# Chaining the token-stationary products of an encoder block on TensorE in program order

## The chip, the cores and the metric

The kernel runs on one core of a Trainium2 chip. The metric is the device time of one execution in microseconds (us), the median of several runs.

## The reference

One layer of a streaming encoder with 256 tokens of width 2048, in float32. What matters here is the sequence of large matrix products:

```python
x = x + 0.5 * swiglu(rms_norm(x), ffn1_w_gate, ffn1_w_up, ffn1_w_down)   # 2048 -> 5632 -> 2048
proj = rms_norm(x) @ w_in                                                # 2048 -> 4112
x = x + concat([pool_mixer(...), gla_mixer(...)]) @ w_out                # 2048 -> 2048
x = x + mem_cross_attention(rms_norm(x), rms_norm(mem), w_q, w_kv, w_o)  # 256 memory tokens
x = x + 0.5 * swiglu(rms_norm(x), ffn2_w_gate, ffn2_w_up, ffn2_w_down)
return rms_norm(x)
```

`swiglu(h, g, u, d)` is `(silu(h @ g) * (h @ u)) @ d`.

## The kernel before

**Precision.** Each float32 operand is split into a high and a low part in the type that TensorE takes at full rate: ScalarE casts the high part (`wh`, L247), VectorE subtracts it from the operand for the low part (`wl`, L248). One float32 product then is three TensorE products: low times high, high times low and high times high. In `products` (L330) the stationary side is 128 tokens of an activation (`act`) and the moving side 512 columns of a weight, so these blocks are called token-stationary.

**Units.** The weights stream through SBUF in units of 1 MB. `Stream` keeps a list of units and of small operations to be put between them (`op(f, after=n)` puts f behind n more units). `emit` walks the list: it splits the weights of the unit that lies two ahead, then traces the products of the present one. There are three buffers each for the raw weights, `wh` and `wl`.

**Two kinds of units in a block.** `block_t` and `block_b` use plain units of 24 products. `block_s`, which makes two column blocks of 512 for all 256 tokens, mixes plain units (`unit_p`, 24 products at L330) with Strassen units (`unit_s`, seven block products P1 to P7 of three TensorE products each, 21 products at L454 in `seven`). For the Strassen units VectorE forms sums of weights (`T`, L431) and of activations (`Sums`). P2, P3 and P4 go straight into the result's sums; P1, P5, P6 and P7 go into two more PSUM tiles that `combine` adds up (L516 to L519) after the last Strassen unit of the block. The first Strassen unit of a block has the order P1, P7, P5, P6, P2, P3, P4.

**PSUM.** All of it is one pool of four tiles of two banks (`ptile`, tag `ps`). A `block_s` takes two for the result (`open_whole`) and two for the parts (`open_parts`, with the first Strassen unit).

**Blocks that add into x.** `into_x` runs two such blocks, b = 0 and 1, for the two halves of the 2048 columns. When the half's sums are complete, `residual` (L699) adds them to x; if a norm follows (`gain` is given), two calls of `fold` per half transpose the new x on TensorE (L722, eight transposes each, into a PSUM tile `px`), and ScalarE (L216) and VectorE (L217) copy that tile out into `xs`, by turns for each quarter of it. For the first half these copies are not tied to the order of the weights' splits. The folds of the first half are put one unit behind the half:

```python
for j in range(2):
    st.op(lambda c=2 * b + j: fold(c, gain), 1)
```

so they stand behind the first unit of the second half. Three calls of `into_x` have folds: the last part of the first layer's down projection (`REST`), `w_out` and `w_o` (both `OUTPUT`). In the second half `OUTPUT` has the units in the order 1, 0, 2, 3, 4, 5, 6, 7, with 0 and 4 Strassen units, and `REST` has 1, 2, 0, 3, 4, 5 with 0 a Strassen unit.

**Who orders the instructions.** The program is traced in the order above, and the framework's scheduler then orders each engine's queue: it plays the program through with its own estimate of durations and gives each engine, whenever it is free, the first instruction in traced order whose inputs are ready by that estimate. An order can be forced: `in_turn(engine, f)` puts an instruction behind the one that it last recorded for this engine (`latest`), without a wait for its end. The splits of the weights are forced so on ScalarE and VectorE, and `among_weights` and `behind_weights` put other operations behind those. TensorE's queue is free: in the kernel before, the scheduler takes a product of a later unit ahead when it finds the next one not ready.

Of the kernel before, what the change touches and what calls it, by code (L numbers as in the profile page):

```python
# [90 lines left out]
def build(ctx, tc, I, out):  # L91
    nc = tc.nc
# [132 lines left out]
    def in_turn(engine, f):  # L225

        if engine in latest:
            with tc.issue_after(latest[engine].ins):
                latest[engine] = f()
        else:  # L230
            latest[engine] = f()
# [93 lines left out]
    def products(ps, act, k, h, wh, wl, first, last):  # L325

        tok = slice(h * P, (h + 1) * P)
        parts = [(act[:, k, 0, tok], wh), (act[:, k, 0, tok], wl), (act[:, k, 1, tok], wh)]
        for i, (a, w) in enumerate(parts):
            nc.tensor.matmul(ps, a, w, start=first and i == 0, stop=last and i == 2)  # L330

    def block_t(srcs, act, evict, delays=(0, 0), amid=None):

        n_k = 2 * len(srcs)
        held = {}

        def unit(gi):
            def fn(wh, wl):  # L340
                if gi == 0:
                    held["ps"] = [ptile(uid("pt")) for _ in range(2)]
                wh, wl = (w.rearrange("p (k j n) -> p k j n", j=2, n=NB) for w in (wh, wl))
                quarters = [(j, kk) for j in range(2) for kk in range(2)]
                if amid is not None and gi == 0:
                    quarters.sort(key=lambda q: q[1])
                for n, (j, kk) in enumerate(quarters):
                    if amid is not None and n == (1 if gi else 3):
                        amid(gi)
                    k = 2 * gi + kk  # L350
                    for h in range(2):
                        products(held["ps"][j][:, h, :], act, k, h, wh[:, kk, j], wl[:, kk, j],
                                 k == 0, k == n_k - 1)
            return fn

        for gi, src in enumerate(srcs):
            st.unit(src, unit(gi))
        for j in range(2):
            st.op(lambda j=j: evict(j, held["ps"][j]), delays[j])
# [80 lines left out]
    def seven(banks, act, sums, g, fresh, ends, weights, order):  # L440
        th, tl, rh, rl = weights
        k0, k1, lo, hi = 2 * g, 2 * g + 1, slice(0, P), slice(P, S)
        a11, a12, a22 = ([act[:, k, p, t] for p in range(2)] for k, t in ((k0, lo), (k1, lo), (k1, hi)))
        s3, n1, n4, s2 = sums.parts(g)
        table = {
            "P1": (a11, rh[:, 0], rl[:, 0]), "P3": (n4, rh[:, 1], rl[:, 1]),
            "P2": (a12, rh[:, 2], rl[:, 2]), "P5": (n1, th[:, 0], tl[:, 0]),
            "P7": (s3, th[:, 1], tl[:, 1]), "P6": (s2, th[:, 2], tl[:, 2]),
            "P4": (a22, th[:, 3], tl[:, 3]),
        }  # L450
        for n in order:
            (a, b), wh, wl = table[n]
            for j, (x, w) in enumerate(((a, wh), (a, wl), (b, wh))):
                nc.tensor.matmul(  # L454
                    banks[n], x, w, start=n in fresh and j == 0, stop=n in ends and j == 2
                )

    def block_s(srcs, act, sums, order, evict, merge=None, sevens=None, late=0):

# [21 lines left out]
        def unit_s(g):  # L481
            def fn(weights):
                if g == sevens[0]:
                    open_parts()
                open_whole()
                fresh = {f"P{i}" for i in range(1, 8)} - seen
                seen.update(fresh)
                ends = ("P1", "P5", "P6", "P7") if g == sevens[-1] else ()
                if "P1" in fresh:
                    order = ("P1", "P7", "P5", "P6", "P2", "P3", "P4")  # L490
                elif merge:
                    order = ("P1", "P2", "P4", "P3", "P5", "P6", "P7")
                else:
                    order = ("P1", "P2", "P3", "P7", "P5", "P6", "P4")
                seven(held["banks"], act, sums, g, fresh, ends, weights, order)
            return fn

        def unit_p(g):
            def fn(wh, wl):
                open_whole()  # L500
                wh, wl = (w.rearrange("p (k j n) -> p k j n", j=2, n=NB) for w in (wh, wl))
                for j in (1, 0):
                    for h in range(2):
                        n = names[j, h]
                        for kk in range(2):
                            products(held["banks"][n], act, 2 * g + kk, h, wh[:, kk, j],
                                     wl[:, kk, j], n not in seen and kk == 0,
                                     g == order[-1] and kk == 1)
                        seen.add(n)
            return fn  # L510
# [35 lines left out]
    def block_b(srcs, act, evict, delay=0):  # L546

        n_k = 4 * len(srcs)
        held = {}

        def unit(gi):
            def fn(wh, wl):
                if gi == 0:
                    held["ps"] = ptile(uid("pb"))
                wh, wl = (w.rearrange("p (k n) -> p k n", n=NB) for w in (wh, wl))
                for kk in range(4):
                    k = 4 * gi + kk
                    for h in range(2):
                        products(held["ps"][:, h, :], act, k, h, wh[:, kk], wl[:, kk],
                                 k == 0, k == n_k - 1)  # L560
            return fn

        for gi, src in enumerate(srcs):
            st.unit(src, unit(gi))
        st.op(lambda: evict(held["ps"]), delay)
# [926 lines left out]
```

## Time and profile before

| | |
|---|---|
| median of 3 runs | 2102.96 us (2101.17 to 2103.69) |
| the profiled execution | 2102.94 us |
| its span, first to last instruction | 2101.2 us |
| mean granted TensorE clock | 0.998 |
| busy: TensorE, VectorE, ScalarE | 99%, 83%, 53% |
| moved from HBM | 417.58 MB, 207 GB/s over the span |

In the lines of a page PE is TensorE, PEld its weight loads, DVE VectorE, ACT ScalarE, SP the queue that issues the weight DMAs. A row of a timeline has the start from the span's beginning, the duration of the row, engine, source line, operation, output and inputs by tile name, how many instructions the row merges, and in brackets the idle time before it with what ended it. A row of the waits has the waiting group, what it waited for, the sum in us, how often, and the longest. A row of a table by windows has the stretch, its length, the busy time and count of PE, PEld, DVE, ACT and POOL, the granted TensorE clock, the busy share of the DMA engines and GB/s.

### The profile page before, as it was taken

The page shows a single profiled execution, that of the slowest core. Times are in us where ns is not written, and L with a number is a line of the kernel's source. Part 1 is how long each engine was busy: PE and PEld are TensorE (multiplying, and loading weights), DVE is VectorE, ACT ScalarE, POOL GpSimd, SP SyncE. Part 2 cuts the span into 40 slices and gives each one's busy share as a digit, 9 for nine tenths or more (in the row PEclk, how much of TensorE's full clock was granted, in tenths as well). Part 3 has the DMA queues.
Part 4 walks back from the last instruction along what each step waited for, and adds up shares of the span by engine and source line. Part 5 has one row for each costly group of instructions (what it writes and reads, how often), then busy time and mean ns, then how long its engine had stood idle before and what let it go on. Part 6 is the DMA issues. An engine that isn't in the chain of part 4 may idle for free.

```text
span 2101.2 us, 24556 instructions
## 1 busy us (share of the span) xinstructions
PE 2084.1 (99%) x9898; PEld 1741.7 (83%) x9898; DVE 1737.5 (83%) x1578; ACT 1118.8 (53%) x1100; POOL 13.1 (1%) x41
## 2 busy tenths in 40 slices
PE   9999999999999999999999999999999999999998
PEld 7878888888888788888888888888888888888886
DVE  7999899989998777678766455779998999989974
ACT  7655455645554545455645444456554556545544
POOL 0000000000000000000000000000000000000001
PEclk9999999999999999999999999999999999999999
DMA  7556666566656565467754555656566755676673
GB/s 261 202 199 224 237 220 216 185 223 249 213 197 236 191 198 183 158 192 242 262 185 161 163 174 165 219 184 227 190 227 211 245 202 191 225 240 220 206 257 118
DMA packets 143608, 435.94 MB, mean 207 GB/s; under 512 B 9860, under 2 KB 13544, under 8 KB 143112
## 3 DMA queue, kind: packets, MB, share of 16 engines
q1 hardware_dynamic: 143464, 434.38, 61.5%
q8 instruction: 77, 1.26, 0.2%
q14 instruction: 35, 0.29, 0.0%
q10 hardware_dynamic: 32, 0.01, 0.0%
HBM read 417.58 MB, written 16.78 MB: 207 GB/s over the span
## 4 chain that ended last, share of the span: by engine, by line
PE 92%; DVE 5%; issue 2%; ACT 1%; DMA 0%; SPq 0%; DVEq 0%; ACTq 0%
PE pt L330 43%; PE pt L454 21%; PE pa L315 14%; PE pb L330 6%; PE pe L330 3%; DVE wl L248 1%; DVE T L431 1%; PE ph L807 1%; DVE wl L435 1%; DVE xl L248 1%; PE pl L1226 1%; PE pv L1261 1%; ACT wh L247 1%; PE px L722 0%; DVE sg L531 0%
## 5 line engine op out<-in xcount | busy, mean ns | idle before, releaser
L248 DVE TENSOR_TENSOR wl<-raw,wh 128x2048 fp32r<-128x2048 f32 (+2 forms) x278 | 624.0, 2250 | 215.8 <-ACT wh L247 215.1
L247 ACT CAST wh<-raw 128x2048 fp32r<-128x2048 f32 (+2 forms) x278 | 521.2, 1880 | 318.5 <-PE pt L330 83.1
L330 PE MATMUL pt<-wh,xs 128*128 128x512 f32 x1536 | 494.9, 390 | 0.1
L330 PE MATMUL pt<-wh,ys 128*128 128x512 f32 x1344 | 423.4, 390 | 0.0
L434 ACT CAST wh<-T 128x1024 fp32r<-128x1024 f32 x208 | 218.8, 1053 | 347.4 <-DVE T L431 340.8
L330 PEld LDWEIGHTS pt<-wh,xs 128*128 128x128 f32 x1536 | 287.5, 188 | 59.4 <-ACT xs L216 0.4
L315 PE MATMUL pa<-xs,wh 128*128 128x512 f32 x896 | 317.4, 399 | 2.7 <-ACT wh L247 2.5
L330 PE MATMUL pt<-wl,xs 128*128 128x512 f32 x768 | 299.7, 390 | 0.0
L330 PEld LDWEIGHTS pt<-wh,ys 128*128 128x128 f32 x1344 | 251.9, 188 | 52.3 <-ACT wh L247 0.4
L330 PE MATMUL pt<-wl,ys 128*128 128x512 f32 x672 | 261.6, 389 | 0.0
L315 PE MATMUL pa<-xs,wl 128*128 128x256 f32 x896 | 248.4, 281 | 0.0
L435 DVE TENSOR_TENSOR wl<-T,wh 128x2048 fp32r<-128x2048 f32 x104 | 237.6, 2285 | 1.0 <-ACT wh L434 0.8
L315 PEld LDWEIGHTS pa<-xs,wh 128*128 128x128 f32 x896 | 168.1, 189 | 41.8 <-ACT wh L247 3.2
L248 DVE TENSOR_TENSOR xl<-raw,xh 128x1536 fp32r<-128x1536 f32 x104 | 182.2, 1752 | 13.6 <-ACT xh L247 13.6
L315 PEld LDWEIGHTS pa<-xs,wl 128*128 128x128 f32 x896 | 169.8, 190 | 2.1 <-issue 0.2
L330 PEld LDWEIGHTS pt<-wl,xs 128*128 128x128 f32 x768 | 144.2, 188 | 29.9
L247 ACT CAST xh<-raw 128x1536 fp32r<-128x1536 f32 x104 | 153.9, 1480 | 24.2 <-PE pt L454 13.4
L431 DVE TENSOR_TENSOR T<-T,raw 128x512 f32<-128x512 f32 x208 | 143.7, 691 | 5.8
L330 PEld LDWEIGHTS pt<-wl,ys 128*128 128x128 f32 x672 | 126.2, 188 | 26.2
L431 DVE TENSOR_TENSOR T<-raw 128x1024 f32<-128x1024 f32 x104 | 126.9, 1220 | 0.5
L454 PE MATMUL pt<-wh,xs 128*128 128x512 f32 x320 | 124.6, 389 | 0.0
L454 PE MATMUL pt<-wh,xe 128*128 128x512 f32 x320 | 124.5, 389 | 0.0
(236 smaller groups left out, 2430.6 us busy)
## 6 DMA issues: line engine op xcount, KB each, us to landing
raw<-in_ffn_w_down SPq DMA_DIRECT2D x88, 1024.0 KB, 5.6
raw<-in_ffn_w_up SPq DMA_DIRECT2D x80, 1024.0 KB, 5.0
raw<-in_ffn_w_gate SPq DMA_DIRECT2D x77, 1024.0 KB, 5.1
raw<-in_w_in SPq DMA_DIRECT2D x32, 1024.0 KB, 5.3
raw<-in_xattn_w_kv SPq DMA_DIRECT2D x32, 1024.0 KB, 5.2
raw<-in_w_out SPq DMA_DIRECT2D x16, 1024.0 KB, 5.7
raw<-in_xattn_w_q SPq DMA_DIRECT2D x16, 1024.0 KB, 5.7
raw<-in_xattn_w_o SPq DMA_DIRECT2D x16, 1024.0 KB, 5.6
```

What stands on the lines that cost most here:

```text
L247: in_turn("scalar", lambda: nc.scalar.copy(hi, src))
L248: in_turn("vector", lambda: nc.vector.tensor_tensor(out=lo, in0=src, in1=f32(hi), op=ALU.subtract))
L315: nc.tensor.matmul(o, w, x, start=k == 0 and i == 0, stop=last and i == 1)
L330: nc.tensor.matmul(ps, a, w, start=first and i == 0, stop=last and i == 2)
L431: in_turn("vector", lambda: nc.vector.tensor_tensor(out=o, in0=a, in1=b, op=ALU.add))
L434: in_turn("scalar", lambda: nc.scalar.copy(th[:, c], t[:, c]))
L435: in_turn("vector", lambda: nc.vector.tensor_tensor(out=tl, in0=t, in1=f32(th), op=ALU.subtract))
L454: nc.tensor.matmul(banks[n], x, w, start=n in fresh and j == 0, stop=n in ends and j == 2)
L807: nc.tensor.transpose(v[:, i, h * P : (h + 1) * P], g[:, h, i * P : (i + 1) * P], ident)
L1226: nc.tensor.matmul(ps[:, t, :M], ys[:, 4 * h + d, a, tok], xa["K"][:, d, b, :], start=i == 0, stop=i == 11,)
L1261: nc.tensor.matmul(ps[:, d, :S], xa["V"][:, m, a, col], xa["PT"][:, m, b, :], start=i == 0, stop=i == 5,)
```

## The change

The products of `products` (called by `block_t`, `block_s`, `block_b` and the last down projection) and of `seven` are queued on TensorE with `in_turn`, each behind the one traced before it. `block_a`, whose stationary side is the weight, the transposes and the attention's products are not touched.

```diff
@@ -327,7 +327,9 @@
         tok = slice(h * P, (h + 1) * P)
         parts = [(act[:, k, 0, tok], wh), (act[:, k, 0, tok], wl), (act[:, k, 1, tok], wh)]
         for i, (a, w) in enumerate(parts):
-            nc.tensor.matmul(ps, a, w, start=first and i == 0, stop=last and i == 2)
+            in_turn("tensor", lambda: nc.tensor.matmul(
+                ps, a, w, start=first and i == 0, stop=last and i == 2
+            ))
@@ -451,9 +453,9 @@
         for n in order:
             (a, b), wh, wl = table[n]
             for j, (x, w) in enumerate(((a, wh), (a, wl), (b, wh))):
-                nc.tensor.matmul(
+                in_turn("tensor", lambda: nc.tensor.matmul(
                     banks[n], x, w, start=n in fresh and j == 0, stop=n in ends and j == 2
-                )
+                ))
```

## The prediction

> **What bounds the kernel now.** I read the page's first and fourth parts, then what TensorE waited for, then the timeline of single engines around the places where units are mixed.
>
> ```profile
> PE 2084.1 (99%) x9898; PEld 1741.7 (83%) x9898; DVE 1737.5 (83%) x1578; ACT 1118.8 (53%) x1100; POOL 13.1 (1%) x41
> ...
> PE 92%; DVE 5%; issue 2%; ACT 1%; DMA 0%; SPq 0%; DVEq 0%; ACTq 0%
> ```
>
> TensorE (PE) is busy 99% of the span and is 92% of the chain that ended last. Whatever makes it stand still is paid in full; VectorE (DVE, 83%) has room on average. What is there to win is what TensorE waited for in the whole span:
>
> ```profile
> PE pa L315 <- ACT wh L247: 2.5, 2, 1.5
> PE pt L454 <- DVE sg L531: 1.6, 4, 1.0
> PE pwarm L186 <- POOL ident masks.py:199: 1.4, 1, 1.4
> PE px L658 <- DMA x<-in_x: 0.9, 1, 0.9
> PE pt L454 <- DVE xl L248: 0.5, 2, 0.3
> PE pa L315 <- DVE xs L217: 0.2, 1, 0.2
> ```
>
> That is 7.1 us. Of it only the two L454 rows, 2.1 us, are waits of the products that the change touches. So the gain has a ceiling of 2.1 us, a tenth of a percent, and all depends on what the mixing of units now hides. Following the order that the program is traced in against the timeline, the largest piece of mixing stands where one half of an output projection ends and the next begins. Here is the output projection `w_out`, TensorE alone:
>
> ```profile
> 967.22 0.39 PE L330 MATMUL pt<-wh,ys 128*128 128x512 f32 x1
> 967.45 0.39 PE L454 MATMUL pt<-xh,ys 128*128 128x512 f32 x1
> ...
> 968.59 1.91 PE L722 MATMUL px<-ident,x 128*128 128x128 f32 x16
> 970.26 0.48 PE L454 MATMUL pt<-xh,ye 128*128 128x512 f32 x1
> ...
> 971.26 0.62 PE L330 MATMUL pt<-wh,ys 128*128 128x512 f32 x2
> ...
> 981.91 0.39 PE L454 MATMUL pt<-xh,ys 128*128 128x512 f32 x1
> ```
>
> The row at 967.22 is the last product of the first unit of the second half. The unit behind it is a seven-product unit (L454). In the program it begins with P1, P7, P5 and P6, which need two new PSUM tiles. The trace instead shows its P2 and P3 from 967.45 on, the 16 transposes of two `fold` calls (L722), P4, and then from 971.26 47 products (L330) of the two units after it; P1 comes at 981.91. The reason is PSUM: there are four tiles, two hold the sums of this half, and the two folds hold the others until ScalarE and VectorE have copied them out:
>
> ```profile
> 967.65 1.91 ACT L247 CAST wh<-raw 128x2048 fp32r<-128x2048 f32 x1 [0.51 <-PE pt L330]
> 969.67 0.47 ACT L216 ACTIVATE xs<-px,gains 128x256 fp32r<-128x256 f32 x1
> 969.59 2.29 DVE L248 TENSOR_TENSOR wl<-raw,wh 128x2048 fp32r<-128x2048 f32 x1 [1.07 <-ACT wh L247]
> 971.80 1.22 DVE L431 TENSOR_TENSOR T<-raw 128x1024 f32<-128x1024 f32 x1
> 972.93 0.87 DVE L217 SCALAR_TENSOR_TENSOR xs<-px,gains,xs 128x256 fp32r<-128x256 f32 x2
> ...
> 976.73 0.88 DVE L217 SCALAR_TENSOR_TENSOR xs<-px,gains,xs 128x256 fp32r<-128x256 f32 x2 [0.15 <-ACT xs L216]
> L217 DVE SCALAR_TENSOR_TENSOR xs<-px,gains,xs x64: 473/480/486, 6.1 to 1406.8; 128x256 fp32r<-128x256 f32 x64
> ```
>
> The last pair starts at 976.73 and one such copy takes 0.48, so the first of the two tiles comes free at 977.21 and the second at 977.61. The scheduler fills these ten microseconds with later units.
>
> **The change part by part.** It adds and removes no operation, no DMA and no semaphore wait by itself: it fixes the order of the products at L330 and L454 among themselves. Transposes, the products at L315 and all other TensorE work stay free. Behind the waiting product on TensorE's queue stand all later products; nobody else can use the gap, since between these units the program has no other TensorE work but the transposes.
>
> *The three folds.* With the chain, P1 follows the unit before it, and only the transposes may come between. They take 1.7 us (968.59 to the next start, 970.26). At this place TensorE then stands from 967.45 + 1.7 = 969.15 to 977.21, 8.1 us. The same structure is at the last down projection of the first feed-forward layer and at the cross-attention output:
>
> ```profile
> 686.84 0.39 PE L454 MATMUL pt<-xh,ye 128*128 128x512 f32 x1
> 691.69 0.87 DVE L217 SCALAR_TENSOR_TENSOR xs<-px,gains,xs 128x256 fp32r<-128x256 f32 x2
> ...
> 694.77 0.88 DVE L217 SCALAR_TENSOR_TENSOR xs<-px,gains,xs 128x256 fp32r<-128x256 f32 x2 [0.15 <-ACT xs L216]
> 1353.17 0.39 PE L454 MATMUL pt<-xh,ys 128*128 128x512 f32 x1
> 1362.46 0.88 DVE L217 SCALAR_TENSOR_TENSOR xs<-px,gains,xs 128x256 fp32r<-128x256 f32 x2 [0.16 <-ACT xs L216]
> ```
>
> The first row of each place is where the next seven-product unit begins now, and P1 would stand there behind the transposes. It would wait from 686.84 + 1.7 to 694.77 + 0.48: 6.7 us, and from 1353.17 + 1.7 to 1362.46 + 0.48: 8.1 us. Together 22.9 us. The transposes come up to 2 us sooner than now, but this does not move the release: ScalarE's first copy stands behind the weight cast that ends at 969.56, VectorE's behind the weight subtraction and the first sum T, and both wait for the end of the same unit as now. Lower bound, if both engines took the copies ahead of weights and sums: half of the transposes (0.85), one copy on ScalarE (0.47), three rounds between the four pairs (691.69 to 694.77, 3.1) and the last copy (0.48) make 4.9 us, 3.2 beyond the transposes' end, 9.6 for three places. Upper bound: one more 1.22 us operation ahead of the copies in each, 26.6. I take 22.9, because it is the queue order that the trace shows.
>
> *The clock after a stop.* A stop of TensorE of this length is not in the trace; the nearest is at the start of the mixer, where it stood for 1.46 and 1.07 us with two products between:
>
> ```profile
> 730.59 0.73 PE L315 MATMUL pa<-xs,wh 128*128 128x512 f32 x2 [1.46 <-ACT wh L247]
> 732.39 1.22 PE L315 MATMUL pa<-xs,wh 128*128 128x512 f32 x2 [1.07 <-ACT wh L247]
> 732.00:736.00 4.00, 3.61 (x12) 3.08 (x13) 4.00 (x3) 2.14 (x2) 0.00 (x0) 0.57 0.48 121
> 736.00:740.00 4.00, 4.00 (x25) 3.48 (x24) 1.54 (x2) 0.77 (x2) 0.00 (x0) 1.00 1.05 395
> ```
>
> The third number from the end is the granted clock: 0.57 over the four microseconds after, then 1.00. So 0.43 x 4 = 1.7 us of TensorE time were lost. I charge this once for each of the three stops: 5.1 us, between 0 and 10.2 (twice as much). The Trainium skill, "TensorE: Matmul & The Clock Gate", Part 1, says that the clock halves after an idle window of about 3.4 us and comes back after a busy one, with windows that run free of the kernel; by that an estimate is 1.7 to 3.4 us a stop, 5.1 to 10.2 in all, where the row alone gives 5.1.
>
> *Block starts elsewhere.* At other starts the scheduler delays P3 behind later products because its PSUM tile is still being read. I put the end of the read beside the place that P3 has in program order. Eight starts show a wait, in the first and in the last of them:
>
> ```profile
> 98.76 0.39 PE L454 MATMUL pt<-xh,xs 128*128 128x512 f32 x1
> 96.92 2.35 DVE L531 TENSOR_TENSOR sg<-pt,sg 128x1024 f32<-128x1024 f32 x2
> 1904.39 0.39 PE L454 MATMUL pt<-xh,xs 128*128 128x512 f32 x1
> 1903.72 1.23 DVE L699 SCALAR_TENSOR_TENSOR x<-pt,x 128x1024 f32<-128x1024 f32 x1
> ```
>
> P3's place is the start of the PE row, the tile comes free at 99.27 and 1904.95: 0.5 and 0.6 us. Eight at 0.5 make 4.0 us; 0 if VectorE's work moves ahead in the slack that the stops give, 13.8 if each waits one 1.23 us operation longer. Where the scheduler now delays the last seven-product unit of a block behind its successor, program order ends it earlier and frees VectorE's combination sooner; I count that as nothing.
>
> *Credit.* After the stops VectorE is ahead, so the 2.1 us of L454 waits may go: the two on `xl` directly follow two of the folds. I credit all of it; it is between 0 and 2.1.
>
> **Sum.** 22.9 + 5.1 + 4.0 - 2.1 = 29.9 us. The profiled execution took 2102.94 us, 1.7 more than its span of 2101.2, and is within 0.1 us of the median 2102.96. Forecast: 2102.9 + 29.9 = 2132.8, rounded 2133 us, slower by 1.4%. A measurement of this kernel can tell about 0.2%, 4.2 us, from no change.
>
> **Rivals.**
> 1. *The folds are served first* (slower, less): VectorE and ScalarE are ordered anew around the new TensorE order and copy the fold tiles before the weights. For it: these copies are not tied to the weights' chain, so the scheduler is free. Against: in the trace it put a weight subtraction and a sum ahead of them, and both inputs are ready no later in the new order. Time: 9.6 + 0 to 4 for blocks + 0 to 2 of clock - 2.1, +7.5 to +13.5: 2110 to 2116. Chance 0.2.
> 2. *The products get clear of the folds* (no loss, perhaps a gain): the scheduler gives the two free PSUM tiles to P1 and P7 first, or moves the transposes a whole unit up, so the stops vanish; TensorE is paid only for block starts, which shrink because the combinations come earlier. Decides at the question who takes the tiles at 960 to 967 us. Against: the transposes stand before P1 in the program, and the trace gives them the tiles first. Time: from -2.1 (the L454 waits gone) to +4.0 (block starts as above), 2100.8 to 2106.9; and if the new order also ended the 2.7 us that L315 waits for `wh` and `xs` (2.5 and 0.2 in the waits), -4.8: 2098.1, the only way to the faster side. Chance 0.1.
> 3. *Late evictions everywhere*: the new order makes the scheduler put PSUM reads behind further weight work at each of the 34 seven-product blocks, one 1.22 us operation each, +41 on top of the folds. Against: most of these reads are chained to the weights by hand. 2150 to 2175. Chance 0.05.
> 4. *The change does nothing*, because the order is already that of the program: excluded by the row at 981.91.
>
> That TensorE would pass a waiting product is no rival: the Trainium skill, same page, Part 2, says matmuls stay in order and only weight loads are pulled ahead; no row here shows one passing.
>
> **How the numbers follow.** Forecast 0.65, the rivals 0.2, 0.1 and 0.05. The forecast's own ends are 9.6 + 0 + 0 - 2.1 = +7.5 and 26.6 + 10.2 + 13.8 = +51, not all at one end together: I take 2118 to 2146 for it. The range reaches down over the first rival: 2109 to 2147. Faster by over 0.2%: 0.04, and within 0.2%: 0.06, the second rival divided; slower: 0.90, the other three.
>
> **What would show it.** Right: in the waits of TensorE three new entries of 6 to 9 us, L454 waiting for VectorE's `xs` copies at L217, at about 688, 976 and 1370 us; a granted clock near 0.5 for some 3 us behind each; P1 directly after the transposes; the page's TensorE share down to 97 to 98%; VectorE and ScalarE busy for the same time as now. Wrong: L217 no longer preceded by L248 and L431 in VectorE's queue (rival 1); no wait over 2 us on TensorE's products (rival 2); waits for L531 or L699 of over 1 us at most block starts (rival 3).

## The result, and the profile after

| | before | after |
|---|---|---|
| median of 4 runs each | 2102.26 us | 2130.83 us (2128.84 to 2131.56) |
| ratio, 95% interval | | 1.0134 (1.0116 to 1.0152) |
| the profiled execution | 2102.94 us | 2128.84 us |
| its span | 2101.2 us | 2127.1 us |
| mean granted TensorE clock | 0.998 | 0.992 |

The changed kernel is slower by 1.34%, 28.6 us by the medians and 25.9 us by the spans of the two profiled executions. In its listings the lines behind the first hunk stand two lower than before: 454 is L456, 531 is L533, 722 is L724.

The page, its busy times and the chain that ended last:

```profile
PE 2088.3 (98%) x9898; PEld 1744.7 (82%) x9898; DVE 1739.6 (82%) x1578; ACT 1118.5 (53%) x1100; POOL 14.3 (1%) x41
...
PE 84%; DVE 10%; issue 3%; ACT 1%; DMA 1%; SPq 0%; DVEq 0%
```

VectorE and ScalarE do the same work in the same time (2.1 us more and 0.3 less). On the chain VectorE's share went from 5% to 10%. What TensorE waited for, in the whole span:

```profile
PE pt L456 <- DVE xs L217: 22.8, 3, 8.0
PE pt L456 <- DVE sg L533: 3.9, 9, 1.0
PE pwarm L186 <- POOL ident masks.py:199: 1.4, 1, 1.4
PE pt L330 <- ACT xs L216: 0.4, 1, 0.4
PE px L660 <- DMA x<-in_x: 0.3, 1, 0.3
```

The sum is 28.8 us, 21.7 more than before. The first row is new and carries all of it: three waits of the Strassen products for the copies of the folds. The two L315 rows of before, 2.7 us at the start of the mixer, are gone. The rest of the 25.9 us is TensorE being busy longer with the same 9,898 instructions: 2088.3 against 2084.1, 4.2 us. The clock, below, accounts for that and for more.

TensorE's timeline at the three places:

```profile
697.03 0.77 PE L456 MATMUL pt<-xh,ys 128*128 128x512 f32 x1 [6.85 <-DVE xs L217]
...
972.76 1.91 PE L724 MATMUL px<-ident,x 128*128 128x128 f32 x16
982.66 0.77 PE L456 MATMUL pt<-xh,ys 128*128 128x512 f32 x1 [7.99 <-DVE xs L217]
983.22 0.63 PE L456 MATMUL pt<-xl,ys 128*128 128x512 f32 x1
...
1367.98 1.91 PE L724 MATMUL px<-ident,x 128*128 128x128 f32 x16
1377.88 0.77 PE L456 MATMUL pt<-xh,ys 128*128 128x512 f32 x1 [7.99 <-DVE xs L217]
```

At the second and third place the 16 transposes are followed directly by P1, which stands for 7.99 us. Before, TensorE did P2, P3, P4 and 47 later products in this time. At the first place the scheduler put the transposes two products ahead of the end of the unit; the stop is 6.85 us. VectorE's queue at the second place shows what P1 waits for:

```profile
974.89 2.29 DVE L248 TENSOR_TENSOR wl<-raw,wh 128x2048 fp32r<-128x2048 f32 x1 [2.04 <-ACT wh L247]
977.10 1.22 DVE L433 TENSOR_TENSOR T<-raw 128x1024 f32<-128x1024 f32 x1
978.24 0.87 DVE L217 SCALAR_TENSOR_TENSOR xs<-px,gains,xs 128x256 fp32r<-128x256 f32 x2
...
981.01 1.89 DVE L217 SCALAR_TENSOR_TENSOR xs<-px,gains,xs 128x256 fp32r<-128x256 f32 x4
```

The transposes are done at 974.67, the first copy of VectorE starts at 978.24, behind a weight subtraction and the first sum of the next unit, and two more sums stand between the copies. The granted clock around the first two places, in stretches of 2 us:

```profile
693.50:695.50 2.00, 0.00 (x0) 0.00 (x0) 1.85 (x4) 0.63 (x2) 0.00 (x0) 0.61 0.19 68
...
699.00:701.00 2.00, 2.00 (x7) 1.57 (x6) 0.00 (x0) 0.00 (x0) 0.00 (x0) 0.56 0.01 3
...
976.00:978.00 2.00, 0.00 (x0) 0.00 (x0) 2.00 (x2) 0.82 (x3) 0.00 (x0) 0.81 0.82 303
...
986.00:988.00 2.00, 2.00 (x7) 1.54 (x7) 0.00 (x0) 0.00 (x0) 0.00 (x0) 0.63 0.00 0
```

If the clock is either 1 or 0.5, a stretch at 0.61 was at 1 for 22% of its time: the drop was at 693.94, and by the row at 0.56 the rise at 700.76. At the second place the same reckoning gives 977.24 and 987.48. So the clock falls some 4 us and 2.5 us into the stop, and stays at half for 3.7 us after TensorE has resumed at 697.03 and for 4.8 us after 982.66. There products follow each other every 0.43 us (983.22 and the rows behind it) and not every 0.227. At the third place the clock is 0.55 from 1373 to 1375 us and 0.64 from 1382 to 1384: it falls at 1373.20 and comes back at 1383.44, 5.6 us after TensorE has resumed at 1377.88.

### The profile page after: what moved, and what is told of

It reads as the page before. It is cut to its first block, busy times and chain, and to the rows that moved or that the text cites. A ratio compares the mean times of both kernels' runs of the same rounds, so it can differ in the third digit from the quotient of the medians.

```text
span 2127.1 us, 24542 instructions
## 1 busy us (share of the span) xinstructions
PE 2088.3 (98%) x9898; PEld 1744.7 (82%) x9898; DVE 1739.6 (82%) x1578; ACT 1118.5 (53%) x1100; POOL 14.3 (1%) x41
## 4 chain that ended last, share of the span: by engine, by line
PE 84%; DVE 10%; issue 3%; ACT 1%; DMA 1%; SPq 0%; DVEq 0%
PE pt L330 39%; PE pt L456 18%; PE pa L315 15%; PE pb L330 6%; PE pe L330 3%; DVE T L433 2%; DVE wl L437 2%; DVE xl L248 2%; DVE wl L248 1%; DMA raw<-in_ffn_w_up 1%; DVE sg L533 1%; ACT wh L247 1%; PE ph L809 1%; PE pl L1228 1%; PE pv L1263 1%
## 5 line engine op out<-in xcount | busy, mean ns | idle before, releaser
L330 PE MATMUL pt<-wh,xs 128*128 128x512 f32 x1536 | 486.4, 390 | 0.4 <-ACT xs L216 0.4
L330 PE MATMUL pt<-wh,ys 128*128 128x512 f32 x1344 | 419.8, 390 | 0.0
L330 PEld LDWEIGHTS pt<-wh,xs 128*128 128x128 f32 x1536 | 287.7, 188 | 59.9 <-ACT xs L216 0.7
L315 PE MATMUL pa<-xs,wh 128*128 128x512 f32 x896 | 315.9, 397 | 0.0
L330 PE MATMUL pt<-wl,xs 128*128 128x512 f32 x768 | 299.3, 390 | 0.0
L330 PEld LDWEIGHTS pt<-wh,ys 128*128 128x128 f32 x1344 | 251.9, 188 | 52.0
L330 PE MATMUL pt<-wl,ys 128*128 128x512 f32 x672 | 261.6, 389 | 0.0
L315 PE MATMUL pa<-xs,wl 128*128 128x256 f32 x896 | 248.5, 281 | 0.0
L315 PEld LDWEIGHTS pa<-xs,wh 128*128 128x128 f32 x896 | 167.5, 188 | 38.1 <-issue 0.3
L315 PEld LDWEIGHTS pa<-xs,wl 128*128 128x128 f32 x896 | 169.1, 189 | 1.7 <-issue 0.2
L330 PEld LDWEIGHTS pt<-wl,xs 128*128 128x128 f32 x768 | 144.2, 188 | 29.9 <-DVE wl L248 0.2
L330 PEld LDWEIGHTS pt<-wl,ys 128*128 128x128 f32 x672 | 126.1, 188 | 26.1
L456 PE MATMUL pt<-wh,xs 128*128 128x512 f32 x320 | 124.7, 390 | 0.1
L330 PE MATMUL pb<-wh,xs 128*128 128x512 f32 x384 | 121.6, 392 | 0.0
```

Source lines behind the costliest of these rows:

```text
L315: nc.tensor.matmul(o, w, x, start=k == 0 and i == 0, stop=last and i == 1)
L330: in_turn("tensor", lambda: nc.tensor.matmul(ps, a, w, start=first and i == 0, stop=last and i == 2))
L456: in_turn("tensor", lambda: nc.tensor.matmul(banks[n], x, w, start=n in fresh and j == 0, stop=n in ends and j == 2))
```

## The experiments

The theory: the loss is three stops, each because the two PSUM tiles of P1, P6, P7 and P5 are held by the folds until their copies are done, plus the clock behind each stop. The rivals: the chain costs a little at every block (late evictions); or the copies' place in the queue is what matters and can be mended; or one hunk alone makes the loss. Each ratio is to the kernel before, on the same chip.

**The chain everywhere but where the folds are.** A flag switches the chain off in the second half of the three blocks with folds.

```diff
-            in_turn("tensor", lambda: nc.tensor.matmul(...))
+            queued(lambda: nc.tensor.matmul(...))   # in_turn, except in those three second halves
```

> The chain of products stays everywhere but in the second half of the three blocks whose first half is followed by folds; there the scheduler may mix units as before. If the loss sits in the folds' PSUM tiles (theory: 22.9 us of stops and about 5 of clock), the three waits of 8 us on L217 are gone and the time is 2099 to 2107 us, that of the kernel before or a few us under it. If the loss comes from queueing products at every block (late evictions, or a cost of the order itself), most of it stays: 2120 us or more, with no wait on L217.

Measured: 2105.94 us, ratio 1.0017 (1.0008 to 1.0027). Within the expected range, and a little slower than before. Its waits:

```profile
PE pt L461 <- DVE sg L538: 4.2, 9, 1.0
PE pa L320 <- ACT wh L252: 2.5, 2, 1.5
```

No wait on L217 at the products. What the chain costs elsewhere is the block starts: 4.2 us in nine waits, where before had 1.6 in four.

**The chain only where the folds are.** The opposite: the kernel before, chained in those three second halves alone.

> The kernel before, with the chain only in the second half of the three blocks with folds. Theory: all of the loss is there, three waits of 6.9 to 8.1 us on L217 and a clock near 0.5 behind each, 2125 to 2133 us. If the loss comes from the chain elsewhere: 2102 to 2107. The two runs together tell whether the parts add up to the whole, 28.6 us.

Measured: 2125.28 us, 1.0109 (1.0092 to 1.0126).

```profile
PE pt L461 <- DVE xs L217: 22.1, 3, 8.0
PE pt L461 <- DVE sg L538: 1.6, 4, 1.0
```

The three stops are here in full, and the block starts are as before. By their spans this kernel is 22.3 us longer than before and the other one 4.2 us; together 26.5, and the whole change is 25.9. By the medians it is 22.5 and 3.2, together 25.7 of 28.6; the 2.9 us between are about the spread of the changed kernel's own four runs (2.7 us). So the parts add up to within that, and about four fifths of the loss is in three half blocks.

**The whole chain with the first Strassen unit later.** Only the order of units in the second halves differs from the changed kernel.

```diff
-    OUTPUT = IntoX(..., (1, 0, 2, 3, 4, 5, 6, 7)), ...
+    OUTPUT = IntoX(..., (1, 2, 3, 0, 4, 5, 6, 7)), ...
-    REST = IntoX(..., (1, 2, 0, 3, 4, 5)), ...
+    REST = IntoX(..., (1, 2, 3, 4, 0, 5)), ...
```

> The whole chain as in the changed kernel; only the order of units in the second halves is changed, so that the first Strassen unit comes as fourth (OUTPUT) or fifth (REST) and not as second or third. Theory: when P1 asks for its PSUM tile the folds have long been copied out, so the three stops vanish with the chain in place: 2098 to 2107 us. If a chained order costs time in itself, whatever takes the tiles: 2120 us or more. If the folds then take their tiles at another place and stop another product, a wait on L217 or L699 of some us shows there, 2108 to 2120.

Measured: 2108.68 us, 1.0030 (1.0018 to 1.0042).

```profile
PE pt L456 <- DVE sg L533: 3.9, 9, 1.0
PE pt L456 <- DVE xl L248: 2.6, 2, 1.3
PE pt L456 <- ACT xh L247: 1.8, 2, 0.9
```

The stops vanish with the chain in place: nearly four fifths of the loss go without touching the chain. The time is 1.7 us over the expected range, and the two new rows say why: in this order the two Strassen units of `OUTPUT` follow each other, and the second one waits for its weight parts `xh` and `xl`, 4.4 us, at both uses of `OUTPUT`.

**The two Strassen units apart.** The order of `OUTPUT` becomes 1, 2, 3, 0, 5, 4, 6, 7.

> As the whole chain with the first Strassen unit later (2108.7 us), but the second Strassen unit of the output projections' second half no longer follows the first directly: order 1, 2, 3, 0, 5, 4, 6, 7. In that run the two stood back to back, and the second waited 0.9 us for xh (L247) and 1.3 us for xl (L248) at both places, with a clock of about half speed behind each. Theory: these 4.4 us and about 2 us of clock go, 2102 to 2104 us, no TensorE wait over 1.4 us. If the waits come from the activation of the folds and not from the neighbour, they stay: 2107 to 2110.

Measured: 2103.52 us, 1.0008 (0.9999 to 1.0016), as expected.

```profile
PE pt L456 <- DVE sg L533: 4.0, 9, 1.0
PE pt L456 <- DVE xs L217: 1.8, 2, 0.9
```

A full chain with units that suit it is level with the kernel before. Of the stops 1.8 us are left.

**The copies of the folds first.** The copies of the first half too are tied behind the weights split so far, ahead of the next unit's split and sums.

```diff
-        among_weights(parts) if c >= 2 else parts()
+        among_weights(parts)
```

> The whole chain; the copies of the folds are tied in program order on ScalarE and VectorE in the first half too, ahead of the next unit's weight split and its sum T. Rival 1 of the prediction made by hand. Theory (the stops are as long as the queue in front of the copies): each stop shrinks from 8 us to 3 to 5 us, together by 9 to 14 us, and the time is 2112 to 2120 us. If the length is set by TensorE's transposes or by the copies themselves, the stops stay at 7 to 8 us and 2127 to 2131 us. If the weights then come late, a wait on wl or wh of a few us appears behind each fold and the time stays over 2122.

Measured: 2123.53 us, 1.0101 (1.0086 to 1.0116). Only 7.3 us better than the changed kernel, and over the expected range. The waits:

```profile
PE pt L456 <- DVE xs L217: 16.4, 6, 3.4
```

Each stop has become two, one for each tile. ScalarE's timeline at the second place shows that the copies are now first, and how long they are by themselves:

```profile
974.34 0.47 ACT L216 ACTIVATE xs<-px,gains 128x256 fp32r<-128x256 f32 x1 [0.91 <-PE px L724]
...
976.39 0.47 ACT L216 ACTIVATE xs<-px,gains 128x256 fp32r<-128x256 f32 x1 [0.55 <-DVE xs L217]
977.42 0.84 ACT L216 ACTIVATE xs<-px,gains 128x256 fp32r<-128x256 f32 x2 [0.55 <-DVE xs L217]
```

ScalarE makes the high part of a quarter, waits 0.55 us while VectorE makes the low part, and goes on: 1.03 us for a quarter, 7.5 us for both tiles, with both engines idle about half of the time. Only between the last quarter of the first tile and the first quarter of the second does it not wait; the row at 977.42 holds both. No wait for `wl` or `wh` has come up behind the folds. So my expectation was wrong: made tile after tile, the copies themselves take nearly as long as the stop.

The run changed more than the place of the copies, however. The tie puts all copies of the second tile behind those of the first. In the kernel before, a round of 1.03 us served a quarter of each tile (the rows with x2 from 691.69 to 694.77), four rounds in all, where this run has seven. A run with the copies ahead of the weights and still in pairs was not made. The Trainium skill, "PSUM — Partial Sum Buffer", section "PSUM bank collisions raise a hardware error", says that two engines that touch the same bank and quadrant have to be kept apart, two readers too. The trace shows more than that asks for: a tile has two banks of two quarters each, and ScalarE waits 0.55 us before the third quarter (976.39) as well, which lies in the other bank. Here the wait goes with the tile; what imposes it, no run shows.

**One hunk at a time.** First only the plain products (L330) chained, then only the Strassen products.

> The kernel before with only the plain products (first hunk) chained. Theory: P1 can still be passed, first by P2, P3 and P4 of its unit and then by the plain products of the next two units, which come in their own order anyway; so no stop: 2100 to 2106 us, no wait on L217 over 1 us. If a chain on one kind of product is enough to stop TensorE: three waits of 4 to 8 us, 2115 us or more.

Measured: 2106.82 us, 1.0020 (1.0011 to 1.0029). No stop at the folds, as expected, but 0.8 us over the range:

```profile
PE pt L330 <- DVE sg L523: 3.1, 4, 0.8
```

Four block starts now wait for the last read of a PSUM tile by `combine`.

> The kernel before with only the Strassen products (second hunk) chained. P1, waiting for a PSUM tile, holds P2, P3 and P4 behind it, but the plain products of the next units may pass: theory 2100 to 2107 us with no wait on L217 over 1 us, and the waits for L531 at block starts as in the kernel before or up to 2.3 us more, if they come from the order inside a Strassen unit. If the Strassen units alone make the stops: 2120 us or more. Together with the run of the first hunk: if both are near 2103, the loss belongs to neither hunk alone but to the two being one chain.

Measured: 2135.88 us, 1.0160 (1.0146 to 1.0174). This is 29 us over the range of my theory, and 5 us above both hunks together by the medians, though the two intervals just overlap:

```profile
PE pt L454 <- DVE xs L217: 23.0, 3, 8.0
PE pt L454 <- DVE wl L435: 4.8, 4, 1.2
PE pt L454 <- DVE sg L531: 4.2, 9, 1.0
```

The second hunk alone makes all three stops, though the plain products are free. The reason I then formed: the plain products add into the same two PSUM tiles as P2, P3 and P4 (the sums of the half), and the scheduler does not let products into one tile change places. In TensorE's queue of the kernel before, 1,859 transposes and products stand ahead of one that was traced before them, but in none of the 262 PSUM tiles do two stand out of traced order. With P2, P3 and P4 chained behind the waiting P1, the plain products are held too, without a chain of their own. The next two runs test this.

**P2, P3 and P4 ahead of P1.** In both, the first Strassen unit of a block has another order; the one has only the Strassen products chained, the other the whole chain.

```diff
-                    order = ("P1", "P7", "P5", "P6", "P2", "P3", "P4")
+                    order = ("P2", "P3", "P4", "P1", "P7", "P5", "P6")
```

> Only the Strassen products chained, as in the run that took 2135.9 us, but the first Strassen unit of a block has the order P2, P3, P4, P1, P7, P5, P6. Theory: there the plain products of the next units did not pass the waiting P1 because they add into the PSUM tiles of P2, P3 and P4, which stood behind P1, and products of one tile never change places. With P2, P3 and P4 ahead of P1 the plain products may pass: the three waits of 7 to 8 us on L217 go, 2102 to 2112 us (block starts keep the 4 to 9 us of waits on sg and wl that the first hunk's absence brings). Rival: whatever stands ahead, a chain of Strassen products stops TensorE until P1 has its tile; then each stop is only 2.0 us shorter (nine products of 0.227 us) and the time is 2127 to 2131 us.

Measured, Strassen products chained alone: 2110.37 us, 1.0036 (1.0022 to 1.0049). Its largest waits:

```profile
PE pa L315 <- ACT wh L247: 2.9, 2, 1.8
PE pt L454 <- DVE wl L435: 2.7, 6, 0.8
PE pt L454 <- DVE xl L248: 2.7, 3, 0.9
```

The stops are gone: 25.5 us less than with the other order of the same products. The reason holds: what P1 stopped were the products of the sums. The 7.8 us that are left to the kernel before are not taken apart here.

> The whole chain, both hunks, with the same order P2, P3, P4, P1, P7, P5, P6 in the first Strassen unit. Theory: with both kinds of products in one chain nothing can pass P1, and the order moves only nine products of 0.227 us ahead of it: three stops of 5 to 6 us, 16 to 17 us in all, and 2123 to 2127 us; the clock's loss behind each stop stays. If the order inside the unit were what makes the stops, they vanish here as well: 2102 to 2110 us.

Measured, whole chain: 2129.20 us, 1.0129 (1.0113 to 1.0144), 2 us over the range.

```profile
PE pt L456 <- DVE xs L217: 16.0, 3, 6.0
PE pt L456 <- DVE sg L533: 6.8, 9, 1.6
```

The stops are as long as expected (22.8 - 3 x 2.0 = 16.8; 16.0 measured). So with both kinds in one chain nothing passes P1. But at the other block starts the waits for a PSUM tile that is still being read grow from 3.9 to 6.8 us, which takes back nearly half of what the shorter stops give. The timeline of the largest shows why: the first product that waits is now P1, with the nine products of P2, P3 and P4 ahead of it, where it was P2 with the twelve of P1, P7, P5 and P6 ahead. So it asks three products, 0.7 us, sooner, and waits 1.60 us in place of 1.00.

**The order of units alone.** The kernel before with the order of units of the run with the units apart, no chain.

> The kernel before, no chain at all, with that order of units (OUTPUT 1, 2, 3, 0, 5, 4, 6, 7; REST 1, 2, 3, 4, 0, 5 in the second halves). Theory: the waits of 2.7 us for wh and xs at the start of the mixer and the 1.7 us of clock behind them go, as in the chained kernel with the later Strassen unit, and the block starts stay at 1.6 us: 2097 to 2100 us, faster than both kernels. If the mixer's start was cured by the chain and not by the order: 2101 to 2104.

Measured: 2105.02 us, 1.0015 (1.0006 to 1.0024): not faster, slower, and above both expected ranges. The waits for `wh` at the mixer's start are longer than in the kernel before (3.3 of the 3.7 us stand there):

```profile
PE pa L315 <- ACT wh L247: 3.7, 3, 2.3
```

**The chain in one half block.** The kernel before, chained in the second half of `REST` alone, with the order 1, 2, 3, 4, 0, 5 there.

> The kernel before with the chain in one block alone, the second half of the first layer's last down projection (REST), and there the order of units 1, 2, 3, 4, 0, 5. The order alone left the waits at the mixer's start (3.7 us for wh), the chain with this order had none. Theory: the chain together with the order cures them, 2.7 us and 1.7 us of clock, and nothing else changes: 2097 to 2100 us, faster than the kernel before by 0.1 to 0.25%. If the chain elsewhere had a part in it: 2101 to 2104 us with the waits for wh in place.

Measured: 2098.07 us (2097.39 to 2099.45, 11 runs), ratio 0.9979 (0.9970 to 0.9988). This is faster than both kernels, as expected. All its waits:

```profile
PE px L672 <- DMA x<-in_x: 1.8, 1, 1.8
PE pt L461 <- DVE sg L538: 1.6, 4, 1.0
PE pwarm L186 <- POOL ident masks.py:199: 1.4, 1, 1.4
PE pt L461 <- DVE xl L253: 0.5, 2, 0.3
```

No wait at the mixer's start is left. The timelines of the four kernels show the difference, in the last product of the block on TensorE and the last residual on VectorE (L699, L701 or L713). Before:

```profile
709.23 0.39 PE L330 MATMUL pt<-wh,ys 128*128 128x512 f32 x1
...
715.99 1.22 DVE L699 SCALAR_TENSOR_TENSOR x<-pt,x 128x1024 f32<-128x1024 f32 x1
```

The order of units alone:

```profile
708.72 0.39 PE L454 MATMUL pt<-wh,ye 128*128 128x512 f32 x1
709.15 1.23 DVE L518 TENSOR_TENSOR sg<-pt,sg 128x1024 f32<-128x1024 f32 x1 [2.72 <-PE pt L454]
...
717.56 2.35 DVE L699 SCALAR_TENSOR_TENSOR x<-pt,x 128x1024 f32<-128x1024 f32 x2
```

The chain in one half block:

```profile
710.25 0.39 PE L335 MATMUL pt<-wh,ys 128*128 128x512 f32 x1
...
711.65 2.35 DVE L713 SCALAR_TENSOR_TENSOR x<-pt,x 128x1024 f32<-128x1024 f32 x2
```

The changed kernel:

```profile
719.75 0.39 PE L330 MATMUL pt<-wh,ys 128*128 128x512 f32 x1
...
718.94 2.46 DVE L701 SCALAR_TENSOR_TENSOR x<-pt,x 128x1024 f32<-128x1024 f32 x2
```

From the start of the last product to the completed x it takes 8.0 us before (715.99 + 1.22 - 709.23), 11.2 with the order alone, 3.8 and 1.7 us in the two chained kernels. The norm and with it the cast of the mixer's first new weights follow: it starts at 728.65 before, at 729.98 with the order alone and at 725.77 with the chain in one half block. With the order alone the block even ends on a Strassen product (L454): the scheduler put Strassen products behind the plain ones, so that their sums were combined late (L518 waits 2.72 us for them). The chain forbids this. None of the seven kernels with both kinds of products chained in this half block waits at the mixer's start (L315); of the six others, all but the one with the Strassen products alone chained do. That is the good side of the change. In the changed kernel it is there too, but a stop of 6.85 us stands in the same half block; the later order takes the stop away.

## Why the prediction was right, point by point

Forecast 2133 us, measured 2130.83. The terms against the rows of the profiled execution:

| term | predicted us | measured us |
|---|---|---|
| three stops at the folds | 22.9 (6.7, 8.1, 8.1) | 22.8 (6.85, 7.99, 7.99) |
| the clock behind them | 5.1 | 7.1 (1.9, 2.4, 2.8) |
| block starts | 4.0 | 2.3 (3.9 - 1.6 at L533) |
| credit at the L454 waits | -2.1 | -0.5 (the `xl` row) |
| mixer's start, waits | 0 | -2.7 |
| mixer's start, clock | 0 | -1.7 |
| program's start, waits at L330 and L660 | 0 | -0.2 (0.4 - 0.6) |
| TensorE's other busy time | 0 | -1.2 |
| sum | 29.9 | 25.9 |

*The stops* came out by the rule that was used: the first product that needs a held tile stands where program order puts it, and the tile's release is where it is in VectorE's queue. Release and reason are shown by the runs with the chain on and off at these places, and by the order of units that clears the tiles first. What the prediction did not see is that, with the unit's own order, the chain of the plain products has no part in the stops; the sums' own tiles order them.

*The clock* is half of the time from TensorE's resuming to the rise of the clock: 3.7, 4.8 and 5.6 us, so 1.9, 2.4 and 2.8. The prediction took 1.7 a stop from a row with shorter stops, and 2.4 on average was measured: this term was too small. TensorE's busy time grew by 4.2 us, which is these 7.1 less the 1.7 that before lost at the mixer, less 1.2 us that stay unexplained. The Trainium skill, "TensorE: Matmul & The Clock Gate", Part 1, gives free-running windows of 3.4 us; the trace agrees: from drop to rise it is 6.82 us at the first place and 10.24 us at the second and the third, two and three windows. The estimate that the prediction took from it, 5.1 to 10.2 us for three stops, holds the measured 7.1.

*Block starts* were put too high, and the waits stand elsewhere than forecast. P3, for which eight waits of 0.5 us were forecast, waits at five starts, 0.16 us each. The other 1.5 us of the 2.3 come from four starts where P2 waited before already, 1.6 us in all then and 3.1 now. *The credit* was wrong: the waits for `sg` did not go but grew, as the chain itself makes them (4.2 us with no stop at the folds). *The mixer's start* was counted as nothing in the sentence on Strassen units that the scheduler delays; it was worth 4.4 us, as rival 2 had priced it in part. So the ceiling of 2.1 us on what the chain could gain was too low as well: chained in one half block it gained 4.5 us. These misses have opposite signs and part of the nearness of 2133 to 2131 is luck of that kind: by the profiled execution, 2128.84, the sum is 4.0 us too high.

*Rival 1* (folds served first) did not happen by itself: the copies still stand behind a subtraction and a sum (978.24). Made by hand it came to 2123.5, not 2110 to 2116: its price took 3.2 us for the copies' part of a stop and 16.4 / 3 = 5.5 was measured, because the tie makes the copies tile after tile and the price has them in pairs. With pairs it was not run. *Rival 2* (clear of the folds) became real with another order of units: 2103.5, within its 2098 to 2107. *Rival 3* (late evictions everywhere, 41 us) is excluded: the chain outside the three half blocks costs 3.2 us by the medians.

## What to carry to other kernels

Before fixing an engine's order, list the places where it passes a waiting instruction now, and what that one waits for; each may become a stop, and its length can be estimated from when the other engine's queue releases the tile (22.9 us forecast and 22.8 measured here). Where an order must be fixed, move the instruction that needs a contended PSUM tile behind work that does not, or take only the place where a fixed order pays: here one half block, with its Strassen unit later, gained 0.2% and the whole lost 1.3%. In this kernel's queue products into one tile are a chain already, and a chain on a few of them can hold all the others.

## What the runs showed of the hardware that was not expected

A stop needn't be empty for the clock to fall. With the first Strassen unit later, TensorE stood for 0.88 and 1.29 us with one product between, and the products behind followed each other every 0.43 us for some 3 us. And the fall can come after the stop: in the run with P2, P3 and P4 ahead and the whole chain, TensorE stood for about 4 us, to 699.8, at the first place, and the windows there read

```profile
697.00:699.00 2.00, 0.00 (x0) 0.00 (x0) 1.73 (x4) 1.68 (x5) 0.00 (x0) 1.00 0.89 288
699.00:701.00 2.00, 1.19 (x5) 1.03 (x6) 0.90 (x3) 0.53 (x2) 0.00 (x0) 0.94 0.99 365
701.00:703.00 2.00, 2.00 (x7) 1.54 (x6) 0.00 (x0) 0.00 (x0) 0.00 (x0) 0.50 0.60 234
```

The clock is full through the stop and half from about 700.8 on, when TensorE is at work again; by the stretch from 703 to 705, at 0.70, it is back at 704.2. So the length of a stop alone does not set the loss. Two stops of the same 7.99 us left 4.8 and 5.6 us of work at half clock, one of about 4 us left 3.4. What is regular is the time from drop to rise: 3.4 us here, 6.82 and twice 10.24 us in the changed kernel, close to one, two and three times the same length.
